# Recurrence of a hybrid decoder trunk: the transfers of its 32x32 systems and inverses get a higher priority in the sync engine's queue

## The chip, the cores and the metric

The kernel runs on one core of one Trainium2 chip. The metric is the time of one execution in device microseconds (us); lower is better. A core has engines that run in parallel, each with an instruction list of its own in a fixed order: TensorE (PE in the profile, with its weight loads as PEld), VectorE (DVE), ScalarE (ACT), GpSimd (POOL) and SyncE (SP). In this kernel every transfer between the memory outside (DRAM) and the memory on the core is issued by SP, in SP's order. A transfer that has to wait for something holds back all transfers behind it in that order.

## The reference, cut to what matters

The program is a two-layer decoder trunk on 272 tokens (16 meta tokens and 256 real ones) of width 2048. Layer 0 mixes tokens with RWKV-7, layer 1 with gated linear attention, each followed by an MLP of hidden width 8192. The change lies in the RWKV-7 part, whose state update is, for each of 32 heads of width 64:

```
def step(S, inp):
    r_t, w_t, k_t, v_t, a_t, b_t = inp
    sa = jnp.einsum('bhvk,bhk->bhv', S, a_t)
    S = S * w_t[:, :, None, :] + sa[..., None] * b_t[:, :, None, :] + v_t[..., None] * k_t[:, :, None, :]
    y = jnp.einsum('bhvk,bhk->bhv', S, r_t)
    return S, y
```

The kernel does not walk token by token. It takes chunks of 64 tokens (four chunks, and a last one of 16 tokens padded to 32). Inside a chunk the term `sa` of one token depends on those of earlier tokens through a triangular system, so a chunk needs the inverse of a unit triangular 64x64 matrix per head.

## The kernel before, in words

**Weights.** Every large product is computed in a split form: a weight block of 128x1024 is loaded into a buffer `raw` (line 132), ACT casts it to `hi` (line 140), DVE computes `lo` = `raw` - `hi` (line 141), and PE multiplies with both. There are three `raw` buffers and two of `hi` and of `lo`. Loads of weights are issued by `wload` under `tc.high_priority(offset=2000)`, so that the scheduler places them early. Lines 163 to 165 are the three products of one 128x128 piece; a block serves eight pieces, 24 matmuls.

**The recurrence.** The heads are handled in two groups of 16, `g` = 0 and 1. The five chunks of a group make two batches: chunks 0 and 1, and chunks 2, 3 and 4; so there are four batches `b` = 0 to 3. For a batch:

- `scores` (line 525) forms the matrices of the chunk on PE, DVE masks them into `AM` (or `AMr` for the short chunk), and the two 32x32 diagonal blocks of each 64x64 system are stored to DRAM in `sysd` (line 531), two transfers for each call. On the way back the heads lie on the partitions, so that the solves of all heads run side by side.
- `invert` loads the systems into `sysA` (line 549, one or two transfers; POOL sets the diagonal at line 550), eliminates on DVE in 30 steps of two operations (`upd`, `sysA`), stores the inverses to `invd` (line 559), transposes a copy on DVE (line 561), and loads the inverted blocks back into `AM` (line 565: four transfers, and a fifth into `AMr` for the short chunk).
- `merge` combines the two 32x32 inverses into the 64x64 one: PE multiplies with the transposed inverse (line 648), ACT copies (line 651), PE multiplies with the inverse that came back from DRAM (line 658), ACT copies the result into `AM` (line 661). Between the two PE parts stand 12 matmuls of ordinary weight work (`R(4)`). Line 658 needs the first and the third of the four transfers of line 565.

There are therefore four merges, of batches 0 to 3, in this order of time. Between the steps of the recurrence PE does the projection `v_proj` and the output products `outQ`, `outA`, `outB`; `R(n)` runs `n` pieces of them. `centre` (line 671) reads the evacuated projection (`hres`, line 816); `norm` (lines 763 to 784) is the group norm of the chunk outputs.

**What sets the order.** In this part the PE's list is written out by hand (`tc.manual_schedule`). The lists of DVE, ACT and SP are made by a scheduler ahead of time: of the instructions that it holds to be ready it takes the one of the highest priority, and priority is program order, moved forward by the offset of `tc.high_priority`. In the batch-0 part (the loop over `f`, lines 567 to 617) the PE's list is made by it too.

Of the kernel before, what the change touches and what calls it, by code (L numbers as in the profile page):

```python
# [54 lines left out]
class Kern:  # L55
# [242 lines left out]
    def rwkv(self, done):  # L298
        nc, tc, ap = self.nc, self.tc, self.ap
# [7 lines left out]
        sysd, invd = ([self.t(self.dp, [112, 32, 32], f"{n}{b}") for b in range(4)] for n in ("sysd", "invd"))  # L307
# [58 lines left out]
        with tc.manual_schedule(engines={ENG.PE, ENG.DVE, ENG.Activation}):  # L366
            for _ in range(2):
                nc.tensor.matmul(idle, warm[:, :128], warm[:, :512], start=True, stop=True)
            for i in range(8):
                sq, h = self.t(ep, [P, 2, T], "x", KT), d[:, 2 * i : 2 * i + 2]  # L370
# [9 lines left out]
            x, o = self.weave(w[:, :512]), self.pairs(idle)  # L380
# [134 lines left out]
        def scores(b, c, e):  # L515
            BK, AR = BKs[c > 1], ARs[c > 1]
            n, np = (C, 4) if c < NC4 else (32, 8)
            o = 128 * (c % 2) if c < NC4 else 256
            cs = slice(o, o + 2 * n)

            pv = [self.ptr().rearrange("p (h m) -> p h m", h=np)[: 2 * n, :, : 2 * n] for _ in range(2)]
            for p in range(np):
                for q in range(2):
                    rows = slice(64 * q, 64 * q + 64)
                    nc.tensor.matmul(pv[q][:, p], BK[rows, 4 * e + p, cs], AR[rows, 4 * e + p, cs], start=True, stop=True)
            dst, mk = (AMs[c > 1][:, c % 2, 8 * e : 8 * e + 8], self.maskA) if c < NC4 else (AMrs[0], self.maskR)
            for q in range(2):
                tt(dst[:, q::2], pv[q], mk.unsqueeze(1).to_broadcast([2 * n, np, 2 * n]))

            for rows, x in blocks(c, slice(8 * e, 8 * e + 8) if c < NC4 else slice(16)):  # L530
                nc.sync.dma_start(sysd[b][rows].rearrange("h s t -> s h t"), x)

        def blocks(c, heads):
            if c == NC4:
                return [(slice(96, 112), AMrs[0][32:64, :, 0:32])]
            o = 16 * (c % 2)
            return [(slice(32 * u + o + heads.start, 32 * u + o + heads.stop),
                     AMs[c > 1][64 + 32 * u : 96 + 32 * u, c % 2, heads, 32 * u : 32 * u + 32]) for u in range(2)]
# [3 lines left out]
        def invert(b):  # L542
            X = sysA
            n = P if b % 2 else 64
            some_rows = [slice(0, 64), slice(96, 112)][: 1 + b % 2]
            if b % 2:
                nc.gpsimd.memset(X[64:96], 0.0)
            for rows in some_rows:
                nc.sync.dma_start(X[rows], sysd[b][rows])
            nc.gpsimd.memset(X[:n].rearrange("p a b -> p (a b)")[:, ::33], 1.0)  # L550
            yield
            for s in range(1, 31):
                k, m = 31 - s, s
                w = self.t(lp, [P, 256], "upd", 1)[:n, : k * m].rearrange("p (a b) -> p a b", a=m)
                tt(w, X[:n, s : s + 1, s + 1 :].to_broadcast([n, m, k]), X[:n, :m, s : s + 1].to_broadcast([n, m, k]))
                tt(X[:n, :m, s + 1 :], X[:n, :m, s + 1 :], w, ALU.add)
                yield
            for rows in some_rows:
                nc.sync.dma_start(invd[b][rows], X[rows])
            for k in (slice(8 * i, 8 * i + 8) for i in range(4)):  # L560
                nc.vector.transpose(t11.rearrange("p c h s -> p s c h")[:, k], X[0:32, k])
                yield
            for c in ((2, 3, 4) if b % 2 else (0, 1)):
                for rows, x in reversed(blocks(c, slice(0, 16))):
                    nc.sync.dma_start(x, invd[b][rows].rearrange("h s t -> s h t"))

        for f in range(KT):
            r = rr[f]
# [42 lines left out]
            if 9 < f < 14:  # L611
                scores(0, (f - 10) // 2, f % 2)
            if f == 13:
                inv = invert(0)
# [283 lines left out]
        with tc.manual_schedule(engines={mybir.EngineType.PE}):  # L898
            R(43)
            for c, e in units1:  # L900
                some(inv, 5)
                R(13)
                scores(1, c, e)
            for g in range(2):
                last = nothing
                if g:

                    last = norm(0)
                    some(last, 1)
                    for c, e in units1:  # L910
                        R(3)
                        some(last, 1)
                        scores(3, c, e)
                    last = norm(1)
# [5 lines left out]
                R(4)  # L920
                next(m)
                inv = invert(2 * g + 1)
                some(inv, 3)
                until(128 + 128 * g)
# [11 lines left out]
                for c in range(5):  # L936
# [32 lines left out]
                    if g == 0 and c == 2:  # L969
                        scores(2, 1, 1)  # L970
                        inv = invert(2)
# [350 lines left out]
```

## Time and profile before

| | |
|---|---|
| time, median of 3 runs | 2404.45 us (2400.09 to 2407.26) |
| the profiled execution's own time | 2402.54 us |
| its span, first to last instruction | 2400.8 us |
| TensorE clock granted, mean | 0.997 |
| PE busy | 2360.9 us, 98% of the span |
| PEld busy | 2244.1 us, 93% |
| DVE busy | 1611.9 us, 67% |
| ACT busy | 1242.4 us, 52% |
| DRAM traffic | 188 GB/s over the span |
| line 531, stores of systems | 34 transfers, between 237.7 and 439.2 us |
| line 549, loads of systems | 6 transfers, 271.5 to 452.8 us |
| line 559, stores of inverses | 6 transfers, 320.9 to 495.5 us |
| line 565, loads of inverses | 18 transfers, 323.8 to 507.1 us |

The profile shows one execution. A row of the timeline has the start and the length in us, the engine (SPq is SP's list of transfer issues), the line, the operation, what is written and read, and a count of merged instructions; in brackets stands how long the engine sat idle before it, and what ended that. A row of the chosen stretches ("windows") has the stretch, its length, and the busy us of PE, PEld, DVE, ACT and POOL, then the granted clock of PE (1.00 is full speed), the share in which the transfer engines were busy, and GB/s.

### The profile page before, as it was taken

Reading aid. Unit: us, or ns where it says so; the run is one execution under the profiler, and the core shown is the slowest. Engines: PE = TensorE matmul, PEld = TensorE weight load, DVE = VectorE, ACT = ScalarE, POOL = GpSimd, SP = SyncE. Lnnn points to the kernel's source line nnn. Section 1 sums busy time; section 2 is a strip of 40 time slices with the busy share of each in tenths; the row PEclk is TensorE's granted clock in tenths of the full one; section 3 lists DMA queues with packets and bytes.
Section 4 is the critical chain, followed back from the end, with each engine's and each line's share of the span. In section 5 each row is a group of like instructions: output and inputs, shape, how many; then the busy total and the mean of one; then the engine's idle time right before and its main releaser. Section 6 shows DMA issues by size and latency. Waiting matters only on the chain. (4 is left out here: it accounts for less than half of the span.)

```text
span 2400.8 us, 48047 instructions
## 1 busy us (share of the span) xinstructions
PE 2360.9 (98%) x19689; PEld 2244.1 (93%) x19689; DVE 1611.9 (67%) x2734; ACT 1242.4 (52%) x1975; POOL 6.6 (0%) x20
## 2 busy tenths in 40 slices
PE   9999999899999999999999999999999999999998
PEld 8888888889999999999999999999999999999997
DVE  8777886858655555555556777767666666666666
ACT  6376644556555445445345556555555445445444
POOL 0000000000000000000000000000000000000000
PEclk9999999999999999999999999999999999999999
DMA  6578864524555555555555554455555555555554
GB/s 210 169 235 293 248 190 146 146 83 163 183 187 193 187 191 191 188 193 186 192 189 190 196 181 167 159 176 193 182 201 200 200 201 200 202 202 202 201 201 169
DMA packets 160732, 455.34 MB, mean 190 GB/s; under 512 B 34112, under 2 KB 50624, under 8 KB 160512
## 3 DMA queue, kind: packets, MB, share of 16 engines
q1 hardware_dynamic: 160512, 452.27, 55.8%
q8 instruction: 154, 2.52, 0.4%
q14 instruction: 66, 0.54, 0.1%
HBM read 433.86 MB, written 18.35 MB: 188 GB/s over the span
## 5 line engine op out<-in xcount | busy, mean ns | idle before, releaser
L141 DVE TENSOR_TENSOR lo<-raw,hi 128x1024 fp32r<-128x1024 f32 (+1 forms) x818 | 927.4, 1140 | 534.1 <-ACT hi L140 525.9
L140 ACT CAST hi<-raw 128x1024 fp32r<-128x1024 f32 (+1 forms) x818 | 794.6, 979 | 939.4 <-PE pj L164 546.8
L163 PE MATMUL pj<-x,hi 128*128 128x272 f32 (+1 forms) x2624 | 748.6, 285 | 1.7 <-DVE hres L300 1.0
L165 PE MATMUL pj<-x,lo 128*128 128x272 f32 (+1 forms) x2624 | 734.5, 280 | 4.3 <-DVE lo L141 4.1
L164 PE MATMUL pj<-x,hi 128*128 128x272 f32 (+1 forms) x2624 | 734.0, 280 | 0.2 <-DVE x L240 0.2
L163 PEld LDWEIGHTS pj<-x,hi 128*128 128x128 f32 x2624 | 498.1, 190 | 10.2 <-issue 3.7
L165 PEld LDWEIGHTS pj<-x,lo 128*128 128x128 f32 x2624 | 498.2, 190 | 7.2 <-DVE lo L141 6.5
L164 PEld LDWEIGHTS pj<-x,hi 128*128 128x128 f32 x2624 | 498.2, 190 | 3.6 <-issue 1.4
L196 PE MATMUL pj<-x,hi 128*128 128x512 f32 x1280 | 419.9, 382 | 0.1
L197 PE MATMUL pj<-x,lo 128*128 128x256 f32 x1280 | 348.8, 273 | 0.0
L196 PE MATMUL pj<-h,hi 128*128 128x512 f32 x1008 | 330.3, 382 | 0.0
L163 PE MATMUL pj<-h,hi 128*128 128x272 f32 (+1 forms) x1040 | 290.1, 279 | 0.0
L164 PE MATMUL pj<-h,hi 128*128 128x272 f32 (+1 forms) x1040 | 290.1, 279 | 0.0
L165 PE MATMUL pj<-h,lo 128*128 128x272 f32 (+1 forms) x1040 | 290.1, 279 | 0.0
L197 PE MATMUL pj<-h,lo 128*128 128x256 f32 x1008 | 274.8, 273 | 0.0
L196 PEld LDWEIGHTS pj<-x,hi 128*128 128x128 f32 x1280 | 241.9, 189 | 34.1 <-DVE x L996 0.4
L197 PEld LDWEIGHTS pj<-x,lo 128*128 128x128 f32 x1280 | 245.7, 192 | 0.3 <-DVE lo L141 0.2
L196 PEld LDWEIGHTS pj<-h,hi 128*128 128x128 f32 x1008 | 190.5, 189 | 26.5
L163 PEld LDWEIGHTS pj<-h,hi 128*128 128x128 f32 x1040 | 196.6, 189 | 0.0
L164 PEld LDWEIGHTS pj<-h,hi 128*128 128x128 f32 x1040 | 196.6, 189 | 0.0
L165 PEld LDWEIGHTS pj<-h,lo 128*128 128x128 f32 x1040 | 196.6, 189 | 0.0
L197 PEld LDWEIGHTS pj<-h,lo 128*128 128x128 f32 x1008 | 193.5, 192 | 0.0
(270 smaller groups left out, 2077.2 us busy)
## 6 DMA issues: line engine op xcount, KB each, us to landing
raw<-mlp_w_d SPq DMA_DIRECT2D x512, 512.0 KB, 3.3
raw<-gla_in_d SPq DMA_DIRECT2D x98, 512.0 KB, 3.2
raw<-w_rkv_d SPq DMA_DIRECT2D x80, 512.0 KB, 3.9
raw<-gla_o_d SPq DMA_DIRECT2D x32, 512.0 KB, 4.3
raw<-w_r_d SPq DMA_DIRECT2D x16, 512.0 KB, 3.3
raw<-rw_oQ_d SPq DMA_DIRECT2D x16, 512.0 KB, 3.2
ard<-ar SPq DMA_DIRECT2D x16, 288.0 KB, 3.4
bkd<-bk SPq DMA_DIRECT2D x16, 288.0 KB, 3.5
```

The lines of the kernel that those rows point to most:

```text
L140: nc.scalar.copy(hi[:, h], raw[:, h])
L141: nc.vector.tensor_tensor(out=lo[:, h], in0=raw[:, h], in1=hi[:, h].bitcast(F32), op=ALU.subtract)
L163: nc.tensor.matmul(out, hi[:, ws], xh, start=first, stop=False)
L164: nc.tensor.matmul(out, hi[:, ws], xl, start=False, stop=False)
L165: nc.tensor.matmul(out, lo[:, ws], xh, start=False, stop=last)
L196: nc.tensor.matmul(wide, hi[:, ws], xt, start=kt == 0, stop=False)
L197: nc.tensor.matmul(one, lo[:, ws], xt[:, 0], start=False, stop=kt == nk - 1)
```

## The change

All four kinds of transfer of `invert` and the stores of `scores` are put under `tc.high_priority(offset=4000)`, above the 2000 of weight loads:

```diff
             for rows, x in blocks(c, slice(8 * e, 8 * e + 8) if c < NC4 else slice(16)):
-                nc.sync.dma_start(sysd[b][rows].rearrange("h s t -> s h t"), x)
+                with tc.high_priority(offset=4000):
+                    nc.sync.dma_start(sysd[b][rows].rearrange("h s t -> s h t"), x)
...
             for rows in some_rows:
-                nc.sync.dma_start(X[rows], sysd[b][rows])
+                with tc.high_priority(offset=4000):
+                    nc.sync.dma_start(X[rows], sysd[b][rows])
...
             for rows in some_rows:
-                nc.sync.dma_start(invd[b][rows], X[rows])
+                with tc.high_priority(offset=4000):
+                    nc.sync.dma_start(invd[b][rows], X[rows])
...
                 for rows, x in reversed(blocks(c, slice(0, 16))):
-                    nc.sync.dma_start(x, invd[b][rows].rearrange("h s t -> s h t"))
+                    with tc.high_priority(offset=4000):
+                        nc.sync.dma_start(x, invd[b][rows].rearrange("h s t -> s h t"))
```

No transfer is added or removed and no work changes. What changes is the lists, and as the scheduler builds all of them together, those of DVE and ACT (and of PE in the batch-0 part) change too. The four added lines shift the line numbers: line 531 is 532 after the change, 549 is 551, 559 is 562, 565 is 569, and every later line is 4 higher (651 is 655, 661 is 665, 816 is 820).

SP's list at the third merge (batch 2), before. `invd_13` holds the inverses of batch 2, `AM_402` is where they go, `sysd_10` and `sysA` are the systems of batch 3, `raw_5956` and so on are weight loads:

```order
L559 DMA invd_13_87<-sysA_1980 64x1024
L549 DMA sysA_1980<-sysd_10_84 16x1024
L132 DMA raw_5956<-rw_oQ_d 128x1024
L132 DMA raw_6058<-rw_oQ_d 128x1024
L565 DMA AM_402_1979<-invd_13_87 32x16x32
L132 DMA raw_6151<-rw_oQ_d 128x1024
L565 DMA AM_402_1979<-invd_13_87 32x16x32 x2
L132 DMA raw_6254<-rw_oQ_d 128x1024
L565 DMA AM_402_1979<-invd_13_87 32x16x32
```

And after:

```order
L562 DMA invd_13_87<-sysA_1980 64x1024
L551 DMA sysA_1980<-sysd_10_84 16x1024
L132 DMA raw_5956<-rw_oQ_d 128x1024
L569 DMA AM_402_1979<-invd_13_87 32x16x32 x4
L551 DMA sysA_1980<-sysd_10_84 64x1024
L132 DMA raw_6058<-rw_oQ_d 128x1024
L132 DMA raw_6151<-rw_oQ_d 128x1024
L132 DMA raw_6254<-rw_oQ_d 128x1024
```

The four loads of inverses stand together, and the load of the next systems follows them; three weight loads that stood before or among them come behind.

At the first merge (batch 0; `invd_11` into `AM_402`, systems of batch 1 in `sysd_8`) SP's list before:

```order
L565 DMA AM_402_1979<-invd_11_85 32x16x32 x2
L132 DMA raw_4216<-w_rkv_d 128x1024
L531 DMA sysd_8_82<-AM_635_3506 32x8x32 x2
L132 DMA raw_4324<-w_rkv_d 128x1024
L565 DMA AM_402_1979<-invd_11_85 32x16x32 x2
L132 DMA raw_4432<-w_rkv_d 128x1024
L531 DMA sysd_8_82<-AMr_3507 32x16x32
L132 DMA raw_4738<-w_rkv_d 128x1024
L549 DMA sysA_1980<-sysd_8_82 64x1024
L549 DMA sysA_1980<-sysd_8_82 16x1024
```

And after:

```order
L569 DMA AM_402_1979<-invd_11_85 32x16x32 x2
L532 DMA sysd_8_82<-AM_635_3506 32x8x32 x2
L569 DMA AM_402_1979<-invd_11_85 32x16x32 x2
L551 DMA sysA_1980<-sysd_8_82 64x1024
L532 DMA sysd_8_82<-AMr_3507 32x16x32
L132 DMA raw_4216<-w_rkv_d 128x1024
L132 DMA raw_4324<-w_rkv_d 128x1024
L551 DMA sysA_1980<-sysd_8_82 16x1024
L132 DMA raw_4432<-w_rkv_d 128x1024
L132 DMA raw_4738<-w_rkv_d 128x1024
```

Here the weight load `raw_4216` moves behind the load of the next systems and behind the store of the last system (`AMr`). ACT's list at the same place, before, with the cast of that weight block (`hi_4218`) ahead of the copies of the merge:

```order
L140 CAST hi_4218<-raw_4216 128x512 x2
L651 COPY rs_4168<-pt_4169 32x256 x2
L651 COPY rs_4168<-pt_4188 32x256 x2
L661 COPY AM_402_1979<-pt_4227 32x8x32 x2
L661 COPY AM_402_1979<-pt_4246 32x8x32 x2
L140 CAST hi_4326<-raw_4324 128x512 x2
L816 COPY hres_72<-pj_4135 128x272
```

And after:

```order
L655 COPY rs_4168<-pt_4169 32x256 x2
L655 COPY rs_4168<-pt_4188 32x256 x2
L665 COPY AM_402_1979<-pt_4227 32x8x32
L140 CAST hi_4218<-raw_4216 128x512 x2
L665 COPY AM_402_1979<-pt_4227 32x8x32
L665 COPY AM_402_1979<-pt_4246 32x8x32
L140 CAST hi_4326<-raw_4324 128x512 x2
L665 COPY AM_402_1979<-pt_4246 32x8x32
L820 COPY hres_72<-pj_4135 128x272
```

Both casts now stand among the copies of line 661, and one of those copies and the evacuation of the projection (`hres`) come behind them.

In the batch-0 part (the loop over `f`), ACT's list at the place of the first systems' store, before (`W`, `iW` and `kn` are computed from a fetched pair `ca`; `hi_3090` is a cast of weights):

```order
L140 CAST hi_3060<-raw_3058 128x1024
L574 ACTIVATE W_1796<-ca_2805 128x272
L575 ACTIVATE iW_2807<-ca_2805 128x272
L578 ACTIVATE kn_2810<-ca_2805,om_k_a_206,vecs_126 128x272
L575 ACTIVATE iW_2902<-ca_2900 128x272
L578 ACTIVATE kn_2905<-ca_2900,om_k_a_206,vecs_126 128x272
L140 CAST hi_3090<-raw_3088 128x1024
```

And after:

```order
L140 CAST hi_3060<-raw_3058 128x1024
L578 ACTIVATE W_1796<-ca_2805 128x272
L140 CAST hi_3090<-raw_3088 128x1024
L579 ACTIVATE iW_2807<-ca_2805 128x272
L582 ACTIVATE kn_2810<-ca_2805,om_k_a_206,vecs_126 128x272
L578 ACTIVATE W_1796<-ca_2900 128x272
L579 ACTIVATE iW_2902<-ca_2900 128x272
L582 ACTIVATE kn_2905<-ca_2900,om_k_a_206,vecs_126 128x272
```

The cast of weights moves ahead of `iW` and `kn`; on SP the two fetches of `ca` (line 572) move behind the first two stores of systems.

## The prediction

> **What bounds the kernel now.** The page first: its span, and the shares of the engines.
>
> ```profile
> span 2400.8 us, 48047 instructions
> PE 2360.9 (98%) x19689; PEld 2244.1 (93%) x19689; DVE 1611.9 (67%) x2734; ACT 1242.4 (52%) x1975; POOL 6.6 (0%) x20
> ```
>
> PE is the bound; a change that removes no PE work can win only PE's idle time or a slow PE clock. The first moved transfer is issued at 237.7 us and the last at 507.1 (table above), so I asked for stretches of 20 us over 220 to 520 and for stretches of 2 us where their clock was below 1.00:
>
> ```profile
> 380.00:382.00 2.00, 2.00 (x11) 2.00 (x12) 0.36 (x1) 1.94 (x5) 0.00 (x0) 0.60 0.22 38
> 382.00:384.00 2.00, 2.00 (x56) 1.75 (x57) 1.28 (x3) 0.51 (x2) 0.00 (x0) 0.54 0.04 10
> 452.00:454.00 2.00, 0.54 (x20) 0.54 (x22) 0.00 (x0) 0.00 (x0) 0.00 (x0) 0.52 0.55 170
> ...
> 456.00:458.00 2.00, 2.00 (x11) 2.00 (x11) 0.27 (x2) 0.15 (x1) 0.16 (x1) 0.50 1.06 269
> ...
> sum 300.00, PE 284.23 PEld 259.08 DVE 225.54 ACT 155.43 POOL 4.41; mean PE 18.95 PEld 17.27 DVE 15.04 ACT 10.36 POOL 0.29
> ```
>
> The last row is the ceiling: 300.0 - 284.2 = 15.8 us of idle PE in the whole recurrence. To that come two places with about half the clock (the number after POOL). What PE waited for there, from the waits of 230 to 560 and the timeline of PE; the second merge is at 377 us, the third at 449:
>
> ```profile
> PE pt L658 <- DMA AM<-invd: 4.4, 2, 3.5
> ...
> 377.60 0.24 PE L658 MATMUL pt<-AM,rs 32*32 32x32 f32 x2
> 378.73 1.19 PE L658 MATMUL pt<-AM,rs 32*32 32x32 f32 x62 [0.89 <-DMA AM<-invd]
> ...
> 449.73 0.24 PE L658 MATMUL pt<-AM,rs 32*32 32x32 f32 x2
> 453.46 1.91 PE L658 MATMUL pt<-AM,rs 32*32 32x32 f32 x62 [3.49 <-DMA AM<-invd]
> 455.30 0.59 PE L163 MATMUL pj<-x,hi 128*128 128x272 f32 x1
> ...
> 460.04 1.09 PE L671 MATMUL pm<-cst,hres 128*64 128x128 f32 x14
> 461.63 0.43 PE L671 MATMUL pm<-cst,hres 128*64 128x128 f32 x2 [0.51 <-ACT hres L816]
> ```
>
> At both merges PE has an inverse loaded too late, 0.89 and 3.49 us, and half clock follows. These are the waits that the change is aimed at.
>
> **The third merge.** SP's list in the timeline, and how long the loads of inverses took there:
>
> ```profile
> 440.60 0.46 SPq L559 DMA_DIRECT2D invd<-sysA  x1
> 443.45 2.68 SPq L132 DMA_DIRECT2D raw<-rw_oQ_d  x2
> 446.23 0.38 SPq L565 DMA_DIRECT2D AM<-invd  x1
> 447.59 0.33 SPq L132 DMA_DIRECT2D raw<-rw_oQ_d  x1
> 447.95 0.97 SPq L565 DMA_DIRECT2D AM<-invd  x2
> ...
> DMA to landing us min/median/max: 3.3/4.5/5.2
> ...
> invd<-sysA SPq DMA_DIRECT2D x4, 256.0 KB, 3.0
> ```
>
> Line 658 needs the third load. It is issued at about 448.5, behind three weight loads that wait for free buffers, and PE goes on at 453.46. After the change only one weight load (443.45) stands ahead. The store of 440.60 lands 3.0 us later, at 443.6, so the four loads go out at about 443.9 to 445.3, half a us apart (two took 0.97), the third at about 444.9. With 3.3 to 5.2 us to landing it is there at 448.2 to 450.1; PE asks at 449.8. Of the 3.49 us I keep 0.2: **-3.3 us**. The half clock then goes as well: line 658 took 1.91 instead of 1.19 us (-0.7), and the 24 matmuls from 455.30 to 460.04 took 4.74 us, where at full clock they start 0.116 us apart:
>
> ```profile
> 448.36 0.28 PE L164 MATMUL pj<-x,hi 128*128 128x272 f32 x1
> 448.48 0.28 PE L165 MATMUL pj<-x,lo 128*128 128x272 f32 x1
> ```
>
> 24 of these and the change of shape are some 2.9 us, so 1.8 us go: together **-2.5 us**. The wait of 0.51 us at 461.63 is for the evacuation `hres`, which stood behind a cast; the new list of ACT has the cast behind it: **-0.5 us**.
>
> Something comes back later. The systems of batch 3 are loaded with the inverses, some 7 us earlier, and DVE, which stood idle, starts on them earlier:
>
> ```profile
> 457.70 0.19 DVE L300 TENSOR_TENSOR upd<-sysA 128x30 f32<-128x30 f32 x1 [5.83 <-issue]
> ...
> 497.41 0.38 PE L163 MATMUL pj<-x,hi 128*128 128x272 f32 x1 [0.66 <-DVE r L300]
> ```
>
> But PE comes 6 us earlier too, and the DVE list now has one `lo` of 1.3 us and one elimination step behind the first group-norm operation that stood ahead of it. DVE is nearly full from there to 497 us, where PE waits 0.66 us for it: I add 1.3 us of work, less what is saved in idle time, **+0.65 us** (bounds 0 and +2).
>
> **The second merge.** The third load was issued at 375.19, behind two weight loads; now the loads follow the store directly, and the third goes out some 2.5 us sooner (-0.89; the bounds are 0 and all of it). The half clock of 380 to 384 goes with it. The two rows above lose 2 x 0.40 and 2 x 0.46 us of clock, 1.7 at most (some 3.4 us at half clock); part of the work there is small matmuls, so I take 1.5: together **-2.4 us**. The weight load that now waits is used late enough: in 230 to 560 us the list of waits has no cast of weights waiting for its load, and 63 us of casts waiting for PE to release their buffer.
>
> ```profile
> 375.19 0.43 SPq L565 DMA_DIRECT2D AM<-invd  x1
> ...
> ACT hi L140 <- PE pj L164: 63.3, 39, 4.2
> ```
>
> That the half clock comes from the wait is read from the merges without one: at the first line 658 had no idle time inside it, and the clock stayed at 1.00.
>
> ```profile
> 335.85 1.20 PE L658 MATMUL pt<-AM,rs 32*32 32x32 f32 x64
> ...
> 280.00:300.00 20.00, 18.25 (x152) 17.71 (x151) 18.79 (x53) 10.65 (x23) 0.00 (x0) 1.00 0.79 255
> ...
> 320.00:340.00 20.00, 18.50 (x292) 16.92 (x290) 13.21 (x26) 9.46 (x21) 0.95 (x1) 1.00 0.70 187
> ```
>
> The Trainium skill, page TensorE: Matmul & The Clock Gate, section "What's actually happening", has the clock halved after at least one idle window of about 3.4 us. The trace differs at the second merge: 0.89 us of idle time between two runs of small matmuls was followed by half clock. By the page the half clock there would not hang on the wait, and the sum below would be 1.5 us smaller.
>
> **The first merge: a cost.** Here nothing waited, but the weight load `raw_4216` moves behind the store of `AMr`, and its cast among the copies of line 661:
>
> ```profile
> 326.90 0.35 SPq L132 DMA_DIRECT2D raw<-w_rkv_d  x1
> 332.71 0.43 SPq L531 DMA_DIRECT2D sysd<-AMr  x1
> ...
> 328.86 1.28 DVE L300 TENSOR_TENSOR AMr<-pt,cst 64x512 f32<-64x512 f32 x2 [0.43 <-PE pt L525]
> ...
> 336.64 1.49 ACT L661 COPY AM<-pt 32x256 f32<-32x256 f32 x4 [0.85 <-PE pt L658]
> 338.55 1.14 ACT L140 CAST hi<-raw 128x512 fp32r<-128x512 f32 x2 [0.42 <-PE pj L164]
> 339.72 0.39 ACT L816 COPY hres<-pj 128x272 f32<-128x272 f32 x1
> ...
> raw<-w_rkv_d SPq DMA_DIRECT2D x80, 512.0 KB, 3.9
> ```
>
> The store of `AMr` can go at 330.2, when DVE has masked it, so `raw_4216` leaves at about 330.6 instead of 326.9 and with the 3.9 us of the page's row is there by 335; its cast now runs at 337.0. Its first matmul stands after line 671, near 340.6, so 3.6 us remain. But ACT now does one copy, this cast (1.1), two copies, the next cast (1.1) and a copy before `hres`: 337.0 + 1.1 + 0.75 + 1.1 + 0.4 = 340.35 instead of 339.72. Line 671 waits for `hres`: **+0.65 us**.
>
> **The batch-0 part: both signs.**
>
> ```profile
> 246.78 0.73 PE L595 MATMUL pu<-kn,cst 128*128 128x272 f32 x2 [1.66 <-DVE kn L591]
> 283.39 0.72 PE L580 MATMUL pm<-sq,cst 128*128 128x272 f32 x2 [1.75 <-ACT sq L577]
> ```
>
> At 246.78 PE waits for `kn`. Two fetches of `ca` now go behind the first stores of systems, about 2 us later, and on ACT a cast of weights of 1.0 us goes ahead of `iW` and `kn`; DVE drops some work ahead of it. I take **+1.5 us** (bounds +0.5 and +3). At 283.39 PE waits for a square on ACT that stood behind an exponential and two more; in the new list these run a round earlier and it follows the cast directly: **-1.5 us** (bounds -1.75 and 0).
>
> **The sum.** -3.3 - 2.5 - 0.5 + 0.65 - 2.4 + 0.65 + 1.5 - 1.5 = -7.4 us. The profiled execution took 2402.54 us; it would take 2395.1. It lies 1.9 us below the median of 2404.45, so against the medians I forecast 2397.0. A difference of 0.3%, 7.2 us, is about what a measurement of this kernel can tell from no change; the forecast lies on that edge.
>
> **The rivals.**
> 1. *The waits move.* Each new wait of 1 to 3 us (246, 340, 497 us) can bring a piece of half clock, 3.4 us long at the second merge, at a price of up to 1.7 us; two of them (3.4) and 1.5 us more of waiting take 5 us of the gain: 2402. For it: DVE is 18.79 us busy of the 20 from 280 to 300, so what comes to it late stays late. Against it: the 1.75 us of waiting at 283 left the clock of that stretch at 1.00.
> 2. *The half clock does not hang on the short wait* at the second merge, the page's rule above: 1.5 us less, 2398.5. Against it: the first merge.
> 3. *Slower: weights starve at the first merge.* SP stands at the load of `sysA` until the store ahead has landed, and at the store of `AMr` until its mask is done, with four weight loads behind. From 335.5 on the load `raw_4216` is too late for 340.6 (3.9 us to landing and 1.1 for the cast). I put it at 330.6; at 5 us over the limit PE waits 5 us, the clock halves twice (3.4), and batch 1 follows on DVE so late that the second merge waits again (5, and its clock kept): about 15 against a gain of 7.4, 2412. Against it: the mask ends at 330.1, 5 us ahead of that, and the store issued at 440.60 was through in 3 us.
> 4. *It does not do what it says:* the loads go earlier but share the transfer engines with the weight load ahead, land after 451, and the third merge keeps 1.5 us and its half clock: 2401.
>
> **How the numbers follow.** My own sum with its bounds 0.52 (2392 to 2400, a little over half of it beyond 7.2 us; more where a run of before had further half clock), rival 1 0.20, rival 2 0.05, rival 4 0.10, rival 3 and other losses 0.13. Faster by over 0.3%: most of the sum's lower half and a part of its centre, and larger gains, 0.45; within 0.3%: the rest of it and rivals 1, 2 and 4, 0.42; slower 0.13. The bottom of the range is the ceiling without what is not touched (15.8 us): 2388.5; the top takes in rivals 1 and 4 and part of rival 3: 2408.
>
> **What would show it.** Right: line 658 of the third merge without a wait over 0.4 us and no half clock from 370 to 460; line 671 of the first merge waiting 1.1 instead of 0.5; a wait of 2.5 to 3.5 us near 246 and none near 283. Wrong: a cast of weights waiting for its load near 334 to 341, half clock at a place where it was 1.00, or a third merge that waits as before.

## The result, and the profile after

The changed kernel takes 2394.82 us in the median of 7 runs (2391.56 to 2397.13); the kernel before, run beside it and counted with its earlier runs, 2400.48 us (7 runs, 2398.47 to 2407.26). The medians differ by 5.7 us. The ratio goes by all runs, not by the medians (the means differ by 7.4 us): 0.9969, 95% interval 0.9957 to 0.9982, so 0.3%, with 4.3 to 10.3 us inside the interval. The forecast was 2397.0 us, a gain of 7.4 us.

The first line of the page of the changed kernel, then its stretches (columns as before: PE, PEld, DVE, ACT, POOL, clock, share of the DMA engines, GB/s; the sum is that over 220 to 520 us):

```profile
span 2395.3 us, 48040 instructions
```

```profile
246.00:248.00 2.00, 1.67 (x7) 1.67 (x8) 2.00 (x8) 1.20 (x4) 0.00 (x0) 0.50 0.86 260
...
380.00:382.00 2.00, 2.00 (x72) 1.96 (x71) 0.00 (x0) 1.33 (x4) 0.00 (x0) 1.00 0.48 186
382.00:384.00 2.00, 2.00 (x70) 1.87 (x69) 1.35 (x3) 1.69 (x5) 0.00 (x0) 1.00 0.01 4
...
452.00:454.00 2.00, 2.00 (x19) 2.00 (x19) 0.38 (x1) 1.07 (x3) 0.00 (x0) 1.00 0.54 160
456.00:458.00 2.00, 2.00 (x16) 1.84 (x15) 1.49 (x6) 1.93 (x5) 0.00 (x0) 1.00 0.03 10
...
sum 300.00, PE 287.31 PEld 261.75 DVE 227.12 ACT 159.07 POOL 4.41; mean PE 19.15 PEld 17.45 DVE 15.14 ACT 10.60 POOL 0.29
```

The half clock of 380 to 384 and of 452 to 459 us is gone, and a new one has come, from 245.5 to 252.3 us. PE is idle for 12.7 instead of 15.8 us. The waits of PE from 230 to 560 us and the places in its timeline (lines 658 and 671 are 662 and 675 in the changed file):

```profile
PE pj L163 <- DVE kn L300: 2.8, 1, 2.8
PE pt L525 <- DVE AM L300: 2.6, 6, 1.0
...
PE pj L163 <- DVE r L300: 1.8, 1, 1.8
PE pm L675 <- ACT hres L820: 1.3, 1, 1.3
...
246.33 0.59 PE L163 MATMUL pj<-x,hi 128*128 128x272 f32 x1 [2.76 <-DVE kn L300]
342.73 0.43 PE L675 MATMUL pm<-cst,hres 128*64 128x128 f32 x2 [1.30 <-ACT hres L820]
379.88 1.20 PE L662 MATMUL pt<-AM,rs 32*32 32x32 f32 x64
423.24 1.16 PE L525 MATMUL pt<-AR,BK 64*128 64x128 f32 x14 [0.43 <-DVE AM L300]
450.25 1.20 PE L662 MATMUL pt<-AM,rs 32*32 32x32 f32 x64
454.36 1.09 PE L675 MATMUL pm<-cst,hres 128*64 128x128 f32 x16
492.60 0.38 PE L163 MATMUL pj<-x,hi 128*128 128x272 f32 x1 [1.77 <-DVE r L300]
```

The wait for `AM<-invd` has left the list: both merges run through. In its place come three larger waits, for `kn` at 246, `hres` at 342 and `r` at 492, and a small one for `AM` at 423. SP's list shows why the third merge runs through: the four loads of inverses stand together, ahead of three weight loads that wait for buffers.

```profile
444.42 1.98 SPq L569 DMA_DIRECT2D AM<-invd  x4
446.44 0.71 SPq L551 DMA_DIRECT2D sysA<-sysd  x1
447.20 5.54 SPq L132 DMA_DIRECT2D raw<-rw_oQ_d  x3
```

To see where time comes and goes I set equal instructions of the two executions beside each other, whose order on PE is the same from the first merge on. The changed kernel stands at: -0.1 us at the scores of batch 0 (235 us), +1.8 at the first merge, +2.6 after its line 671, +2.3 at the second merge, -0.4 after it, +0.5 at the third merge, -5.7 after it, -5.9 at 477, -4.8 at 497. So the second merge gives 2.7 us, the third 6.2 up to the first matmul of its line 675 (another 0.9 comes within that line, and 0.7 has gone again by 477 us), and batch 0 (-1.9), the first merge (-0.8), the stretch between the second and third merge (-0.9) and DVE near 492 (-1.1) take 4.7 back; 0.3 us between the first and the second merge and 0.2 between the third and 477 us go the other way. These are differences of two single executions; how much of them is the order's own, the experiments have to tell.

### The profile page after: what moved, and what is told of

The parts are those of the page before. It is cut to its first block, busy times and chain, and to the rows that moved or that the text cites. A ratio compares the mean times of both kernels' runs of the same rounds, so it can differ in the third digit from the quotient of the medians.

```text
span 2395.3 us, 48040 instructions
## 1 busy us (share of the span) xinstructions
PE 2359.4 (99%) x19689; PEld 2242.3 (94%) x19689; DVE 1609.9 (67%) x2734; ACT 1241.8 (52%) x1975; POOL 6.6 (0%) x20
```

## The experiments

In all of them the priority is written in line, so that line numbers are those of before. Each kernel was compared with runs of the kernel before on the same chip. Gains in us are differences of medians; the ratios go by all runs, so the two can differ by 1 or 2 us.

**Only the inverses first.** The priority on two lines alone:

```
-                nc.sync.dma_start(invd[b][rows], X[rows])
+                with tc.high_priority(offset=4000): nc.sync.dma_start(invd[b][rows], X[rows])
...
-                    nc.sync.dma_start(x, invd[b][rows].rearrange("h s t -> s h t"))
+                    with tc.high_priority(offset=4000): nc.sync.dma_start(x, invd[b][rows].rearrange("h s t -> s h t"))
```

> Only the stores and loads of the inverses (lines 559 and 565) take priority; the stores and loads of the systems (531 and 549) stay as before. Theory (the gain lies in the loads of inverses alone, the loss of 1.8 us ahead of the first merge comes from the stores of systems of batch 0, which push a fetch of ca back): the wait near 246 us is 1.66 us at full clock as before, the wait of 0.89 us at the second merge and that of 3.49 us at the third go with their half clock (-3.0 and -6.2 us), line 671 of the first merge keeps its 0.5 us, some 0.9 us comes back on DVE at 420 to 447 us: about -8 us against before. Rival (the systems must be stored and loaded early too, or the inverses are not ready in time): the third merge keeps a wait over 1.5 us and its half clock, about -3 us.

2399.57 against 2400.67 us, ratio 0.9989 (0.9980 to 0.9998): 1.1 us by the medians, 2.6 by the ratio, far from the theory's 8. The rival's 3 lies within the interval, but not for its reason: no wait stayed at the third merge. The merges did what the theory said: against the profile of before the kernel won 2.7 us at the second and 6.2 at the third. But it lost 5.1 us after that, from -5.6 at 477 us to -0.5 at 501. SP, DVE and PE of this kernel, and below DVE's first elimination step in the changed kernel:

```profile
446.11 6.29 SPq L132 DMA_DIRECT2D raw<-rw_oQ_d  x3
452.44 0.46 SPq L549 DMA_DIRECT2D sysA<-sysd  x1
...
459.91 0.18 DVE L300 TENSOR_TENSOR upd<-sysA 128x30 f32<-128x30 f32 x1
...
496.71 0.35 PE L163 MATMUL pj<-x,hi 128*128 128x272 f32 x1 [3.23 <-DVE r L300]
```

```profile
455.24 0.18 DVE L300 TENSOR_TENSOR upd<-sysA 128x30 f32<-128x30 f32 x1
```

The larger part of batch 3's systems is still loaded behind three weight loads, 6 us after the inverses. DVE starts the elimination at 459.9 although PE is early, and PE waits 3.23 us for it, with half clock behind. The step I had wrong: I took the early load of systems for a cost (+0.65), but here its absence costs more than its presence.

**Only the stores of systems first** (line 531 alone).

```
-                nc.sync.dma_start(sysd[b][rows].rearrange("h s t -> s h t"), x)
+                with tc.high_priority(offset=4000): nc.sync.dma_start(sysd[b][rows].rearrange("h s t -> s h t"), x)
```

> Only the stores of the systems (line 531) take priority. Theory: this is the part that costs; the fetch of ca lands a microsecond later, PE waits 2.5 to 3 us near 246 us with half clock behind it, the second and third merge wait 0.9 and 3.5 us as before: +1 to +3 us against before. Rival (the half clock near 246 us is an accident of that one execution, and earlier stores help the later inversions): within 1 us of before, no half clock near 246.

2408.83 us, ratio 1.0030 (1.0019 to 1.0041): 8.2 us slower. The wait near 246 us came as expected, 3.06 us with half clock. More came at the second merge, which neither theory had:

```profile
376.88 0.82 SPq L531 DMA_DIRECT2D sysd<-AM  x2
377.80 0.40 SPq L565 DMA_DIRECT2D AM<-invd  x1
...
386.31 1.91 PE L658 MATMUL pt<-AM,rs 32*32 32x32 f32 x62 [5.18 <-DMA AM<-invd]
```

The stores of batch 2's systems now stand ahead of the loads of batch 1's inverses. SP goes past them only at 376.9, and PE, with all loads behind, waits 5.18 instead of 0.89 us. In the full change the loads have the same priority and go first. The stores' priority alone is harmful at two places.

**The change, with the fetch of `ca` ahead of everything.**

```
-            nc.sync.dma_start(ca.rearrange("p a t -> p (a t)"), cad[f])
+            with tc.high_priority(offset=6000): nc.sync.dma_start(ca.rearrange("p a t -> p (a t)"), cad[f])
```

> The change, and the fetch of ca (line 572) ahead of everything on SP (offset 6000). Theory (the fetch of ca behind two stores of systems makes the wait near 246 us and its half clock): both go, the lead at the first merge is 1.5 us or more better than with the change, the rest stays: -7 to -9 us against before. Rival (PE waits there for the vector engine's own list, in another order because of the change): a wait over 2 us and half clock near 246 stay, about -5.5 us.

2398.01 us, ratio 0.9984 (0.9975 to 0.9992): 2.7 us by the medians, short of both; by the ratio 3.8, and the rival's 5.5 is still within the interval. PE waits 2.43 us for `kn` all the same (first row), with half clock after it, but for another reason: DVE cannot write the next `bk`, since the store of the last one has now been pushed back (second row).

```profile
249.83 1.02 PE L595 MATMUL pu<-kn,cst 128*128 128x272 f32 x2 [2.43 <-DVE kn L591]
...
247.30 0.42 DVE L300 TENSOR_TENSOR bk<-kn,iW 128x256 f32<-128x256 f32 x1 [1.33 <-DMA bkd<-bk]
```

It does not settle whether the fetch made the wait in the changed kernel. It shows that SP's order in batch 0 has no slack: what goes ahead delays a transfer that PE's chain needs as well. The fetches go first in every round of the loop, and at 235 us this execution was already 6.2 us behind the profile of before; how much of that is the order's, one profile does not tell.

**Late stores**: the change, with line 531 first only from batch 2 on.

```
-                nc.sync.dma_start(sysd[b][rows].rearrange("h s t -> s h t"), x)
+                with tc.high_priority(offset=4000) if b >= 2 else ExitStack(): nc.sync.dma_start(sysd[b][rows].rearrange("h s t -> s h t"), x)
```

> The change, but line 531 takes priority only from batch 2 on, so that the stores of batch 0 and 1 stand as before. Theory: the wait near 246 us is 1.66 us at full clock and line 671 of the first merge waits 0.5 us as before; the second and third merge gain 3.0 and 6.2 us; the loads of batch 3's systems go early, so 0.5 to 1.1 us comes back on DVE near 490 us, which the kernel with only the inverses first does not pay: -6.5 to -8 us against before, about 1 us behind that one. Rival (the costs ahead of the first merge are taken up by the wait for DVE at 420 to 447 us, so that undoing them wins nothing): -5.5 us, like the change.

2393.72 us, ratio 0.9965 (0.9954 to 0.9977): 7.0 us, the theory's case. Against the profile of before PE stands at 0.0 us at the first merge and -2.7 after the second, it wins 6.2 at the third, and stands at -8.5 after that and -7.6 at the wait near 490.

```profile
247.18 0.72 PE L595 MATMUL pu<-kn,cst 128*128 128x272 f32 x2 [1.67 <-DVE kn L591]
377.56 1.20 PE L658 MATMUL pt<-AM,rs 32*32 32x32 f32 x64
489.84 0.38 PE L163 MATMUL pj<-x,hi 128*128 128x272 f32 x1 [1.79 <-DVE r L300]
```

Line 671 of the first merge waits 0.50 us again, so that the 0.8 us lost there come from the early stores of batches 0 and 1. Between this kernel and the change the intervals overlap; only the places in the profile separate them.

**Only the loads first** (lines 549 and 565; all stores as before).

```
-                nc.sync.dma_start(X[rows], sysd[b][rows])
+                with tc.high_priority(offset=4000): nc.sync.dma_start(X[rows], sysd[b][rows])
...
-                    nc.sync.dma_start(x, invd[b][rows].rearrange("h s t -> s h t"))
+                    with tc.high_priority(offset=4000): nc.sync.dma_start(x, invd[b][rows].rearrange("h s t -> s h t"))
```

> Only the loads take priority: those of the systems (line 549) and of the inverses (565); every store stays as before. It differs from the kernel with only the inverses first by line 549 in place of 559. Theory (what that kernel lacked is the early load of batch 3's systems: its vector engine fell 3.2 us behind at 497 us with half clock after it): no wait over 2 us near 490 us and no half clock there, the second and third merge without a wait, nothing new ahead of 330 us: -6 to -8 us against before, like the kernel with late stores (-7.0). Rival (that loss was an accident of the one execution, and the stores of the later systems carry the gain): -1 to -3 us, with 3 us of wait near 496.

2393.96 against 2401.06 us, ratio 0.9970 (0.9959 to 0.9982): 7.1 us. The wait near 490 is 1.80 us at full clock, as in the kernel with late stores. Two of the four lines carry the whole gain. What the first experiment lacked was the load of systems.

**The first pair of stores as before**, the rest as in the change.

```
+                with tc.high_priority(offset=4000) if (b, c, e) != (0, 0, 0) else ExitStack(): nc.sync.dma_start(sysd[b][rows].rearrange("h s t -> s h t"), x)
```

> The change, but the first two stores of systems (batch 0, chunk 0, half 0), the ones that went ahead of two fetches of ca, stay as before. Theory (the loss ahead of the first merge comes from these two alone): 1.7 us of wait near 246 us at full clock, while line 671 of the first merge still waits 1.3 instead of 0.5 us; the lead at the first merge is +0 to +0.5 us instead of +1.8, the end -6.5 to -7.5 us against before. Rival (it comes from the later stores of batch 0 as much): +1.5 us or more at the first merge, -5.5 us at the end.

2395.41 us, ratio 0.9972 (0.9963 to 0.9982): 5.7 us by the medians, as the rival had it, and 6.7 by the ratio, as the theory had it; the time does not decide. The profile speaks for the theory:

```profile
235.74 1.35 PE L525 MATMUL pt<-AR,BK 64*128 64x128 f32 x16 [2.26 <-DMA BK<-bkd]
248.16 0.73 PE L595 MATMUL pu<-kn,cst 128*128 128x272 f32 x2 [0.85 <-DVE kn L591]
```

Near 246 PE waits 0.85 us at full clock, and from 240 us to the first merge it loses nothing (+2.2 and +2.0 us against the profile of before). What it is behind by comes from a wait of 2.26 us for `BK` at 235 and the half clock after it, where the order is still that of before; other executions wait there 0.3 to 2.0 us. That the two stores alone make the wait near 246 is likely by this one profile; the time does not show it.

**Systems ahead of inverses.** The kernel with late stores, and the load of batch 3's systems ahead of the four loads of inverses.

```
-                with tc.high_priority(offset=4000): nc.sync.dma_start(X[rows], sysd[b][rows])
+                with tc.high_priority(offset=6000 if b == 3 else 4000): nc.sync.dma_start(X[rows], sysd[b][rows])
```

> The kernel with late stores (531 only from batch 2 on), and the load of batch 3's systems ahead of the four loads of inverses (offset 6000 for that one load). In the kernel with late stores the vector engine stands idle for 2.5 us at 450 us, with the first elimination steps listed behind an addition that waits for hres, and PE waits 1.8 us for it at 490. Theory (the vector engine's chain of elimination steps sets that wait): the steps start 2 to 3 us earlier, the wait at 490 us falls below 0.5 us, -8 to -9 us against before. Rival (group norms and low halves of weights, which the earlier steps push back, become late instead, or the inverses load 0.5 us later and the third merge waits): no better than -7 us.

2394.75 us, ratio 0.9972 (0.9962 to 0.9982): 6.3 us, as the rival had it. There is no wait near 490 left, but a cast on ACT came late and PE waits for it, 1.22 us, at another place. DVE and PE of this kernel, then DVE's same step in the kernel with late stores:

```profile
448.35 0.21 DVE L300 TENSOR_TENSOR sysA<-sysA,upd 128x58 f32<-128x58 f32 x1
...
466.86 0.35 PE L163 MATMUL pj<-x,hi 128*128 128x272 f32 x1 [1.22 <-ACT hi L140]
```

```profile
453.15 0.22 DVE L300 TENSOR_TENSOR sysA<-sysA,upd 128x58 f32<-128x58 f32 x1
```

The step runs 4.8 us earlier, of which 1.0 us is PE's own lead.

Its one profiled execution was the shortest of the profiled ones, its median was not: no version tried is faster than the change by more than the measurement can tell.

**Three times the small matmuls.** The kernel with late stores, line 658 of the second merge issued three times.

```
-                for h in range(8):
+                for h in list(range(8)) * (3 if b == 1 else 1):
```

> The kernel with late stores, and the 32x32 matmuls of line 658 at the second merge issued three times each (the same result): 3.4 instead of 1.2 us of small matmuls on end, without any wait. Theory A (what halves the clock is a window of low activity, in which 32x32 matmuls count for little; the wait of 0.89 us in the kernel before only made such a stretch longer): half clock for 3.4 us within 380 to 386 us, and PE 2.3 + 1.0 to 1.7 us behind the kernel with late stores from there on. Theory B (only a PE that stands still counts): clock 1.00 throughout, 2.3 us behind.

```profile
378.60 3.23 PE L658 MATMUL pt<-AM,rs 32*32 32x32 f32 x192
...
380.00:382.00 2.00, 2.00 (x118) 1.96 (x111) 0.00 (x0) 0.86 (x3) 0.00 (x0) 1.00 0.79 315
```

3.23 us of 32x32 matmuls on end left the clock at 1.00 (2397.57 us in its one run), as theory B has it, though a stretch as the clock counts them (last section) held only 2.5 us of them. PE fell 2.0 us behind the kernel with late stores there, and the wait for `AM` of 0.43 us near 423 vanished, so 0.4 us of it came back: the vector engine sets the pace there within half a us.

**From batch 2 on**: all four lines first for batches 2 and 3 alone (`with tc.high_priority(offset=4000) if b >= 2 else ExitStack():` on each).

> All four lines take priority from batch 2 on only, so that the first and second merge stay as before and the third and fourth are as in the change. Theory: the wait of 0.9 us at the second merge and its half clock come again, the third merge wins 6.2 us by itself, some 1 us goes back on the vector engine near 490 us: -4 to -5.5 us against before. Rival for the second merge (its half clock in the one profile of before was an accident, not a consequence of the wait): the wait comes again and the clock stays at 1.00 from 377 to 386 us.

2402.13 against 2400.83 us, ratio 1.0005 (0.9997 to 1.0014): no gain, a miss. The stores of batch 2's systems again went ahead of the loads of batch 1's inverses, which have no priority here:

```profile
384.16 1.91 PE L658 MATMUL pt<-AM,rs 32*32 32x32 f32 x62 [5.12 <-DMA AM<-invd]
```

The second merge lost 4.8 us by that, the third won 5.8 against the profile of before, DVE near 498 took 1.1. It could not say anything on the half clock behind the wait of 0.9 us, for which it was made.

**Before once more.**

> The kernel before once more, for a second profile of it. If the waits and half clocks belong to the order of the instructions: 0.9 us of wait and half clock behind it at the second merge, 3.5 us and half clock at the third, none at 246 and 283 us, where the waits stay between 1.4 and 1.9 us. If half clock after waits of this size is a matter of chance: one of these places comes out the other way.

One run, 2398.8 us. Rows of PE and its stretches:

```profile
378.19 1.19 PE L658 MATMUL pt<-AM,rs 32*32 32x32 f32 x62 [1.01 <-DMA AM<-invd]
451.43 1.19 PE L658 MATMUL pt<-AM,rs 32*32 32x32 f32 x62 [3.41 <-DMA AM<-invd]
...
378.00:382.00 4.00, 3.81 (x130) 3.64 (x132) 0.92 (x2) 2.98 (x7) 0.00 (x0) 1.00 0.55 135
382.00:386.00 4.00, 4.00 (x76) 3.68 (x70) 2.02 (x4) 1.18 (x2) 0.00 (x0) 1.00 0.53 151
454.00:458.00 4.00, 4.00 (x30) 3.87 (x30) 0.98 (x5) 0.81 (x2) 0.16 (x1) 0.67 0.56 143
```

The waits came again, 1.01 and 3.41 us. The half clock of the second merge did not, and that of the third was shorter. The waits near 246 and 283 were 0.93 and 0.92 us, below what I had expected of them.

**The change once more.**

> The changed kernel once more (the same order; the lines written so that their numbers are those of before), for a second profile. If the loss ahead of the first merge belongs to the order: a wait over 2 us near 246 us with half clock behind it, line 671 of the first merge 1.3 us late, no wait at the second and third merge, 1.8 us of wait near 492. If it was that execution's accident: under 1.8 us near 246 and no half clock there.

One run, 2398.64 us. At 235 us it is already 4.2 us behind the profile of before, lost in a part whose order the change does not touch: PE waited 3.54 us there for one square (also in the last section).

```profile
249.58 0.38 PE L163 MATMUL pj<-x,hi 128*128 128x272 f32 x1 [1.70 <-DVE kn L300]
```

Neither forecast held: 1.70 us of wait, not 2.76, and half clock behind it all the same (from 249.92 us; rows in the last section). Between 235 us and the first merge this execution gained 0.5 us on the profile of before, where the other lost 1.9; before's own second profile gained 0.6 there. The remaining places are as in the first profile: 1.30 us for `hres`, 0.43 for `AM`, 1.80 for `r`, no wait at the merges.

## Why the prediction was right, and where it was not

The forecast, 2397.0, was 2.2 us above the measured 2394.82, and its gain of 7.4 was 1.7 more than the medians show and just what the means show. The median of the 3 runs it was set against, 2404.45, lay 4 us above that of more runs. That the total comes so close is in part luck: the third merge gave 0.8 us more than said, and 0.9 us near 423, which the sum does not have, went the other way. By its own steps:

- **Third merge, -3.3 - 2.5 - 0.5.** Right in mechanism and size. The loads of inverses were issued at 444.4 to 446.4 us, as worked out (443.9 to 445.3), line 662 ran without a wait, line 675 waits for no `hres`, and equal instructions gained 6.2 us up to line 675 and 7.1 with that line, against the 6.3 of the sum. The half clock is the part that varies: it was 6.8 us long in the first profile of before (from 452.1 us) and 3.4 in the second (from 453.2), where line 658 took 1.19 us at full clock.
- **Second merge, -2.4.** The wait of 0.9 went, as said. The half clock of 1.5 us came in one of two profiles of before: after 1.01 us of wait at the same place the clock stayed at 1.00. None of the nine profiles without this wait has half clock there, but the wait alone does not bring it, so the second rival had a point, worth 1.5 us in one execution of two. The Trainium skill's page TensorE: Matmul & The Clock Gate, section "What's actually happening", has the window run free of the kernel, which fits two executions of one order that come out differently.
- **The clock terms together.** -2.5 and -1.5 took 4.0 us of lost clock off. The mean granted clock of the runs tells what they were worth: 0.9969 in the 59 runs of before beside the experiments and 0.9983 in the 7 of the change, which times their length is 7.4 and 4.1 us lost. So some 3 us of the gain is clock, not much less than the sum had, though a single profile does not show it.
- **First merge, +0.65.** `hres` came after one copy, a cast, two copies, a cast and a copy, just as counted from ACT's order. It measured 1.30 - 0.50 = +0.8.
- **DVE later, +0.65.** 1.77 - 0.66 = +1.1, within the bounds. The first experiment showed what I had not: without the early load of the systems it would be 3.2 us.
- **Batch 0, +1.5 - 1.5.** The square near 283 us no longer waits: right. The step that failed is the other one: I put +1.5 on the wait near 246 and left the clock out of the sum, because 1.75 us of waiting at 283 had left it at 1.00. The wait was 2.76 and 1.70 us in two profiles, 1.1 and 0.0 more than the 1.66 of before, and in both half clock followed: the first rival, in one place of three. It does not come in every run: three of the seven have a mean clock of 0.999, and the profiles without any half clock but that at the kernel's end have 0.998 to 0.999. Batch 0 as a whole came to +1.9 and -0.5 us against the profile of before in place of nothing. Executions in which PE, ACT and DVE have the order of before differ there by nearly as much (-1.0 to +1.1 us in seven), so a cost of about 1 us is what these few profiles make likely, and it isn't settled.

What made the wait 2.76 us in the first profile shows in SP, ACT and DVE of the changed kernel:

```profile
237.89 0.83 SPq L532 DMA_DIRECT2D sysd<-AM  x2
238.77 0.92 SPq L576 DMA_DIRECT2D ca<-cad  x2
...
242.90 0.43 ACT L578 ACTIVATE W<-ca 128x272 f32<-128x272 f32 x1 [2.24 <-DMA ca<-cad]
243.24 1.03 ACT L140 CAST hi<-raw 128x1024 fp32r<-128x1024 f32 x1
...
244.71 1.22 DVE L141 TENSOR_TENSOR lo<-raw,hi 128x1024 fp32r<-128x1024 f32 x1
245.85 0.43 DVE L300 TENSOR_TENSOR kn<-pj,kn 128x272 f32<-128x272 f32 x1
```

The fetch is issued behind the two stores, 2.3 us after its place in before (236.44), and the exponential starts 1.1 us later than there. Then a cast of 1.0 us stands ahead of `kn` on ACT, and a `lo` of 1.2 on DVE ahead of the product that frees PE's bank. Each was named in the prediction, but they do not add up: the wait grew by 1.1 us, by as much as the exponential was late. In the second profile of the change, counted from 235 us, the fetch was issued 2.1 us later than in before, yet the exponential started only 0.1 us later, and the wait did not grow; with the stores alone it was 1.5 us late, and the wait grew by 1.4; in the second profile of before it was 0.7 us early, and the wait was 0.7 us shorter. So in these executions the wait goes with the landing of the fetch, which differs between executions of one order; the cast and the `lo` ahead show no price of their own.

- **Not in the sum:** the pace of DVE near 423 us. PE, earlier by 3 us after the second merge, ran into it and gave 0.4 us back there in a wait and 0.9 in all up to the third merge.
- The third rival (weights starve at the first merge) did not come: no wait there for a load of weights. The fourth did not come either.

## What to carry to other kernels

A priority in a queue is worth what the wait behind it is worth, and it has to be given to every load that the stages behind it wait for. Here the two kinds of load carry the whole gain, and the stores, when they alone have it, push the loads back and cost 5 us at one merge. Before a second stage is taken for a cost, look at what the first makes early: the third merge's gain was kept only because the next systems came early too. Half clock behind a wait of 1 to 2 us comes in one execution and not in the next, so one profile cannot price it; a second profile of the same kernel, and the mean granted clock of many runs, can.

## What the runs showed of the hardware

How unsure half clock behind a wait is. Of the waits of PE of 1.99 us and more from 100 to 560 us, twelve in thirteen profiles, eleven were followed by it (1.99 to 5.18 us); the longest but two, in the second profile of the change, was not, while one of 1.70 us in the same execution was:

```profile
169.85 0.72 PE L580 MATMUL pm<-sq,cst 128*128 128x272 f32 x2 [3.54 <-ACT sq L577]
...
164.59:168.00 3.41, 1.73 (x15) 1.52 (x14) 2.10 (x4) 0.69 (x2) 0.00 (x0) 1.00 0.55 173
168.00:171.42 3.42, 1.56 (x11) 1.49 (x12) 1.67 (x7) 2.68 (x7) 0.00 (x0) 1.00 0.83 303
171.42:174.83 3.41, 3.41 (x28) 3.25 (x27) 3.41 (x10) 3.15 (x8) 0.00 (x0) 1.00 0.13 25
246.51:249.92 3.41, 1.71 (x22) 1.39 (x21) 3.31 (x12) 3.10 (x7) 0.00 (x0) 1.00 0.73 244
249.92:253.34 3.42, 3.42 (x15) 3.07 (x14) 3.42 (x14) 1.11 (x3) 0.00 (x0) 0.50 0.89 286
```

After waits of 1.66 to 1.85 us it came three times (1.69, 1.70, 1.85) and stayed away in all others, eight of them of 1.77 to 1.81 us near 490; after 0.89 us it came, after 1.01 at the same place it did not.

The traces show more of the reason than the lengths of the waits. In each of the thirteen the granted clock changes only at whole multiples of 3.413 us from its first record (in the profile of before at 380.42, 383.83, 452.10 and 458.93 us), and the multiples lie elsewhere in each execution; the stretches above are cut at them. Counted by these windows, from 20 to 2380 us and at full clock, each of the eight in which PE stood idle for 1.9 us or more was followed by half clock; of the fifteen with 1.6 to 1.9 us, six were; of all others one, that of the second merge of before. The wait of 3.54 us was split into 1.69 and 1.85 us by a border at 168.00. The Trainium skill's page on the clock gate, in the section named above, asks for an idle window of about 3.4 us; here 1.9 us idle within one window was enough. That the window runs free of the kernel, as that page says, agrees with these traces.

What decides between 1.6 and 1.9 us stays open, and so does the second merge of before: its window, 377.00 to 380.42, held 0.89 us of idle time and 1.4 us of 32x32 matmuls, while in the second profile of before a border at 378.13 lay between the wait and most of them. Small matmuls without a wait are not enough: 2.5 us of them in one window (from 379.36 us, in the kernel with three times as many) left the clock alone. No run tested the two together.
